# A second pair of tiles for the scan's solve, and context residual rows that stay on chip between output projection and second norm

## The chip, the core and the metric

The kernel runs on one core of a Trainium2 chip. TensorE multiplies matrices into PSUM, VectorE (DVE), ScalarE (ACT) and GpSimd (POOL) work on tiles of up to 128 partitions in on-chip memory, and SyncE (SP) issues nearly all transfers between that memory and DRAM. Each engine has a queue of its own that it takes in order, and an instruction waits until the tiles it reads are written and the buffer it writes is given back. The metric is the device time of one execution, the median of three runs.

## What is computed

Two layers of a generator's backbone. Each normalises the latent stream (1024 tokens) and the context stream (256 tokens), projects to four mixers (an RWKV-7 scan in both directions, pooling, a Fourier mixer, a convolution), concatenates and projects back, adds the gated result to the residual, normalises again, and applies a SwiGLU feed-forward block. The second layer needs no context output.

```python
def step(S, inp):                      # the scan, per token, head and direction
    w_t, kk_t, a_t, k_t, v_t = inp[:5]
    sa = jnp.einsum('bhvk,bhk->bhv', S, -kk_t)
    S = (S * w_t[:, :, None, :] + sa[..., None] * (kk_t * a_t)[:, :, None, :]
         + v_t[..., None] * k_t[:, :, None, :])
    y = jnp.einsum('bhvk,bhk->bhv', S, inp[5]) if with_out else None
    return S, y
...
    h = h + gt1 * _mix_and_project(ux, y_rwkv_x, *other)
    h = h + gt2 * _swiglu(_modulate(h, norm2_g[l], sh2, sc2), ffn_w_in[l], ffn_w_out[l])
    if not last:
        hc = hc + mc[2] * _mix_and_project(uc, y_rwkv_c, *other)
        hc = hc + mc[5] * _swiglu(_modulate(hc, norm2_g[l], mc[3], mc[4]), ffn_w_in[l], ffn_w_out[l])
```

All matrix products in FP32 are made of three matmuls of a high and a low half each.

## The kernel before

Activations lie as 128 channels by tokens: tb 0 and 1 are the latent's two halves of 512 tokens, tb 2 is the context's 256. The scan is cut into ten stages of 128 tokens a layer (two of context, eight of latent). A stage has a *preparation* (decays by L921 on POOL and the running sum L926 on VectorE, then L942, L947, L950, L956 and POOL's L943, L957, L971), the matmuls *rX* and their masking (L991, four a stage), and the *solve*. The solve inverts small triangular matrices: their entries go from the masked tiles to DRAM (eight stores to Ad, L995) and come back spread over all partitions into two tiles As[0] and As[1] (two loads, L1001). L1029 sets the diagonal on POOL, L1031 to L1035 start the solve on VectorE (As[0]) and POOL (As[1]), and L1043 to L1052 run over eight blocks on VectorE, blocks 0 to 3 from As[0], 4 to 7 from As[1]. The result goes by DRAM (Td, L1056, loaded by L1062) to the *merge* (L1102 and matmuls into pb), and then a chain of small matmuls (pc) and copies carries the state. In the text a stage n runs from the start of solve n to that of solve n + 1, and holds the preparation and the rX for solve n + 1.

Beside the scan `fill()` supplies work: the rest of the input projection, the Fourier mixer, and then the output projection `outp` for tb 2, 1 and 0 (the latent's without the scan's two channel blocks, which are added later). `outp` loads its y tiles from ymix (six for the latent, L1657), splits each into halves (cast L324 on ScalarE, subtraction L325 on POOL), and for each of eight column blocks loads weights and the residual r, runs 18 matmuls of 128x512 into a pf tile (24 of 256 columns for the context), evicts with gate and residual on VectorE (L1684) and stores to ho (L1685). After it `norm2c()` loads the context's eight finished rows back from ho into hc (L1348), takes their squares (L339) and their norm, and the context's feed-forward block follows.

What sets the order: the program is written as interleaved generators, and a scheduler then orders each engine's queue in a simulated time of its own. A tile is given a buffer from a pool; nearly all tiles of 128x512 or less come from one pool, t2, of 73 buffers, and an instruction can be placed only once a buffer is free in that reckoning. A ring `s.rg(R, name, depth)` holds `depth` t2 buffers through a scan.

Of the kernel before, what the change touches and what calls it, by code (L numbers as in the profile page):

```python
# [19 lines left out]
NK = 8  # L20
# [72 lines left out]
class _Kernel:  # L93
# [879 lines left out]
    def inner(s, R, F):  # L973

        nc = s.nc
# [5 lines left out]
        for d in range(2):  # L981
            s.lab(f"rX.{F.seg}{F.i}")
            psh = [s.ps(), s.ps()]
            for u in range(4):
                for h in range(2):
                    rows = slice(64 * h, 64 * h + 64)
# [8 lines left out]
                    nc.sync.dma_start(Ad[b, d, :, h].rearrange("u j i -> j u i"), W[r0:r0 + 32, :, 32 * b:32 * b + 32])  # L995
            yield

        As = [s.rg(R, f"As{a}", 1) for a in range(2)]
        Adf = Ad.rearrange("b d u h j i -> (b d u h) (j i)")
        for a in range(2):  # L1000
            nc.sync.dma_start(As[a], Adf[:, a * 512:(a + 1) * 512].unsqueeze(0).broadcast_to([4, 32, 512]))  # L1001
# [36 lines left out]
        for b in range(8):  # L1038
            x, r0, m = As[b // 4][:, :], 4 * b, b + 1
            o = (r0 % 16) * 32 + r0  # L1040
            with s.ahead(SPRI):
# [3 lines left out]
                n = 28 - r0  # L1045
# [210 lines left out]
    def run(s, nlayers):  # L1256
        nc = s.nc
# [26 lines left out]
        r = [s.norm_r(h, 0, sq="c2")]  # L1284
# [15 lines left out]
        for l in range(nlayers):  # L1300
            last = l == L - 1
# [22 lines left out]
            def fill():  # L1324
                for x in s.rest(l, R, acts, segs):
                    s.mod_step()
                    yield x
                assert not s.mods
                R.rest2 = True
                yield from s.four2(R, segs, swB, ymix)  # L1330
                while not R.sided or not (last or R.ctx):
                    yield None
                for tb in tbs[::-1]:
                    yield from s.outp(l, tb, hd, ho, ymix)
                if not last:
                    yield from norm2c()
                    for f in range(NC):
                        yield from s.ffn1_ctx(l, f, [a[2] for a in acts2], hid[f])

            def norm2c():  # L1340

                for _ in range(2):
                    yield
                s.lab("norm2")
                hc = s.rows(NK, ("c",))
                for k in range(NK):
                    h2[k][2] = hc[k][2]
                    nc.sync.dma_start(hc[k][2], ho[k][:, 1024:1280])  # L1348
                yield
                r = yield from s.rstd_g([h2[k][2] for k in range(NK)], 256, D, 0, False, "ps", lambda j: s.t2())  # L1350
                for k in range(NK):
                    acts2[k][2] = s.act_row(("c",))[2]
                for _ in s.norm_g(l, 1, h2, 2, acts2, r):
                    if _ % 2:
                        yield
# [289 lines left out]
            else:  # L1645
                break

    def outp(s, l, tb, hi_, ho, ymix):

        nc = s.nc  # L1650
        seg, _, n = TBS[tb]
# [20 lines left out]
        for cb in range(NK):  # L1672
            s.lab("outp")
            w = s.wload(s.I["wout"][l, cb], ks[0] * 128)
            r = s.t2()[:, :n]
            nc.sync.dma_start(r, hi_[cb][:, 512 * tb:512 * tb + n])
            ps = s.ps("pf")
            for i, ((wh, wl), (ah, al)) in enumerate(zip(w, acts)):
# [213 lines left out]
```

## Time and profile before

| what | us |
|---|---|
| median of three runs | 3343.46 (3340.38 to 3346.46) |
| the profiled execution's own time | 3351.38 |
| its span, first to last instruction | 3349.6 |
| TensorE busy, matmuls | 3000.7 |
| VectorE busy | 2109.8 |
| ScalarE busy | 1257.5 |
| POOL busy | 1385.8 |

The mean granted clock of TensorE was 0.911 of full speed. Times in the rows are counted from the start of the span. Layer 0's scan runs from about 370 to 910 us, layer 1's from about 2100 to 2600.

### The profile page before, as it was taken

To read this page: it belongs to the slowest core of one execution; us is meant where nothing else is said; L and a number is where in the kernel's file an instruction comes from. 1 tells how busy PE (TensorE), PEld (TensorE's weight loads), DVE (VectorE), ACT (ScalarE), POOL (GpSimd) and SP (SyncE) were. 2 spreads that over 40 slices of the span, in tenths; PEclk is the share of its full clock that TensorE was granted. 3 is DMA by queue.
4 is the path that set the end of the run, shared out by engine and by line. 5 is a ranking of instruction groups with operands and counts; after the bars stand their busy time and mean duration, and the time that the engine had idled before them with its cause. 6 is when DMAs were issued, how large, how long until landed. Compare 5 with 4: busy or idle time off the path is not lost.

```text
span 3349.6 us, 52386 instructions
## 1 busy us (share of the span) xinstructions
PE 3000.7 (90%) x18888; PEld 2410.5 (72%) x18888; DVE 2109.8 (63%) x3498; ACT 1257.5 (38%) x2575; POOL 1385.8 (41%) x1484
## 2 busy tenths in 40 slices
PE   6989997877889999999999978988877799999998
PEld 3657765766678888888888766756665588888787
DVE  6679666666374988644545598666665755554535
ACT  4446433443363222223212455333443433333212
POOL 2366224563168554435310064245550454545400
PEclk8989887787899999999999988987787799999999
DMA  7422344465455444337412212345553322224312
GB/s 265 165 92 97 102 117 136 124 174 156 144 190 164 149 132 151 125 98 233 139 35 78 87 53 90 117 134 139 156 159 88 128 92 79 82 89 164 123 39 78
DMA packets 375818, 415.48 MB, mean 124 GB/s; under 512 B 115587, under 2 KB 214916, under 8 KB 375558
## 3 DMA queue, kind: packets, MB, share of 16 engines
q1 hardware_dynamic: 375558, 412.13, 39.4%
q8 instruction: 149, 2.44, 0.3%
q14 instruction: 111, 0.91, 0.1%
HBM read 306.49 MB, written 100.27 MB: 121 GB/s over the span
## 4 chain that ended last, share of the span: by engine, by line
PE 55%; DVE 14%; DMA 9%; issue 3%; SPq 1%; ACT 1%; POOL 1%; DVEq 0%; POOLq 0%; ACTq 0%
PE pc L153 17%; PE ps L153 17%; PE pb L153 14%; PE pf L153 8%; DMA t<-Ad 3%; DVE c L532 2%; DMA Td<-t 1%; DVE t L1050 1%; DVE t L947 1%; DVE t L1043 1%; DVE f L325 1%; DVE t L956 1%; DVE t L1469 1%; DMA t<-ho 1%; DVE t L1493 1%
## 5 line engine op out<-in xcount | busy, mean ns | idle before, releaser
L153 PE MATMUL pc<-t,f 128*128 128x512 f32 (+1 forms) x3108 | 754.4, 392 | 41.3 <-ACT t L427 16.0
L153 PEld LDWEIGHTS pc<-t,f 128*128 128x128 f32 x3108 | 581.6, 195 | 182.9 <-ACT t L427 20.5
L153 PE MATMUL ps<-t,f 128*128 128x512 f32 (+1 forms) x2094 | 517.0, 393 | 18.4 <-ACT t L324 7.7
L153 PE MATMUL pb<-t,f 128*128 128x512 f32 (+1 forms) x2094 | 470.5, 370 | 8.4 <-ACT t L1468 4.9
L153 PEld LDWEIGHTS ps<-t,f 128*128 128x128 f32 x2094 | 390.8, 190 | 99.8 <-ACT t L324 8.2
L153 PEld LDWEIGHTS pb<-t,f 128*128 128x128 f32 x2094 | 370.4, 190 | 78.8 <-ACT t L1468 6.0
L1515 ACT CAST f<-c 128x512 fp32r<-128x512 f32 x316 | 196.0, 621 | 536.7 <-PE ps L153 132.0
L1517 POOL TENSOR_TENSOR f<-c,f 128x512 fp32r<-128x512 f32 x135 | 186.5, 1381 | 426.2 <-ACT f L1515 411.7
L153 PE MATMUL pf<-t,f 128*128 128x512 f32 (+2 forms) x1500 | 314.2, 364 | 14.2 <-DVE t L1044 4.0
L324 ACT CAST f<-m 128x512 fp32r<-128x512 f32 (+1 forms) x236 | 134.7, 576 | 436.3 <-PE pb L153 226.4
L153 PEld LDWEIGHTS pf<-t,f 128*128 128x128 f32 (+1 forms) x1500 | 249.5, 198 | 61.4 <-ACT f L324 4.4
L530 POOL TENSOR_TENSOR c<-c,cp 128x352 f32<-128x352 f32 (+2 forms) x168 | 183.3, 1092 | 145.9 <-ACT c L523 71.3
L1517 DVE TENSOR_TENSOR f<-c,f 128x512 fp32r<-128x512 f32 x181 | 158.6, 878 | 134.8 <-ACT f L1515 134.4
L153 PE MATMUL pf<-c,f 128*128 128x512 f32 (+1 forms) x704 | 200.5, 416 | 30.0 <-DVE t L1684 20.3
L325 POOL TENSOR_TENSOR t<-c,t 128x512 fp32r<-128x512 f32 (+1 forms) x110 | 135.1, 1266 | 173.8 <-PE ps L153 99.5
L153 PE MATMUL ps<-t,t 64*128 64x128 f32 (+2 forms) x1032 | 159.9, 341 | 38.9 <-DVE t L956 23.4
L532 DVE SCALAR_TENSOR_TENSOR c<-c,dv,c 128x352 f32<-128x352 f32 (+2 forms) x238 | 190.5, 829 | 2.0
L153 PEld LDWEIGHTS ps<-t,t 64*128 64x128 f32 (+1 forms) x1032 | 133.6, 231 | 60.4 <-issue 20.4
L153 PEld LDWEIGHTS pc<-t,t 128*64 128x64 f32 (+2 forms) x2484 | 124.6, 161 | 71.8 <-issue 28.6
L153 PE MATMUL pc<-t,t 128*64 128x64 f32 (+3 forms) x2484 | 156.2, 258 | 20.9 <-DMA t<-t 11.8
L153 PEld LDWEIGHTS pf<-c,f 128*128 128x128 f32 x704 | 131.5, 214 | 60.1 <-issue 19.1
L261 DVE SCALAR_TENSOR_TENSOR cp<-m,sc,cp 128x512 f32<-128x512 f32 x140 | 137.5, 1003 | 43.0 <-DMA m<-in_wmod 42.3
(256 smaller groups left out, 4731.3 us busy)
## 6 DMA issues: line engine op xcount, KB each, us to landing
c<-in_ffin SPq DMA_DIRECT2D x176, 256.0 KB
m<-in_wmod SPq DMA_DIRECT2D x116, 256.0 KB
t<-rw SPq DMA_DIRECT2D x232, 128.0 KB
hid<-t SPq DMA_DIRECT2D x88, 256.0 KB
c<-hid SPq DMA_DIRECT2D x88, 256.0 KB
m<-in_ffout SPq DMA_DIRECT2D x80, 256.0 KB
t<-in_wmod SPq DMA_DIRECT2D x76, 256.0 KB
m<-in_win SPq DMA_DIRECT2D x64, 256.0 KB
```

The lines of the kernel that those rows point to most:

```text
L153: s.nc.tensor.matmul(o, l, r, start=start, stop=stop)
L261: nc.vector.scalar_tensor_tensor(acc[t], w, sc, acc[t], ALU.mult, ALU.add)
L324: r = s.nc.scalar.copy(hi, src)
L325: (eng or s.lo_eng).tensor_tensor(lo, src, hi.bitcast(F32), ALU.subtract)
L530: nc.gpsimd.tensor_tensor(g, g, t_, ALU.add)
L532: nc.vector.scalar_tensor_tensor(a, w[:, j:j + m], tap(j), a, ALU.mult, ALU.add)
L947: nc.vector.scalar_tensor_tensor(KRv[:, :, p, 0, 1:64], k2[:, :, p, 1:64], -2.0, P2[:, :, p, 0:63], ALU.mult, ALU.mult)
L956: nc.vector.tensor_tensor(BKv[rows, :, :, 1 - h, :], cv(kd)[rows], cv(iP)[rows], ALU.mult)
L1043: nc.vector.tensor_tensor(tv, at(x, o, [0, m], [1, 4], [32, 4]), at(T_, r0, [32, m], [0, 4], [1, 4]), ALU.mult)
L1050: nc.vector.tensor_tensor(tv, at(x, o + 4, [0, m], [1, n], [32, 4]), at(T_, r0, [32, m], [0, n], [1, 4]), ALU.mult)
L1515: nc.scalar.copy(hi, x)
L1517: (nc.gpsimd if s.nw % 7 in LOP else nc.vector).tensor_tensor(lo, x, hi.bitcast(F32), ALU.subtract)
```

## The change

`inner` takes As[0] and As[1] from rings of depth 2 in place of 1: two more t2 buffers are held through each scan. In `fill()` the context's four tiles of two rows each (`hc`) are taken before the output projection, and `outp` for the context writes its residual straight into them, in place of eight r tiles of its own; `norm2c` then finds the rows there, without the eight loads and the `yield` behind them. The store to ho stays. Lines behind the change count one less (L1684 becomes L1683, L1657 becomes L1656).

```diff
@@ -995,7 +995,7 @@
                     nc.sync.dma_start(Ad[b, d, :, h].rearrange("u j i -> j u i"), W[r0:r0 + 32, :, 32 * b:32 * b + 32])
             yield
 
-        As = [s.rg(R, f"As{a}", 1) for a in range(2)]
+        As = [s.rg(R, f"As{a}", 2) for a in range(2)]
         Adf = Ad.rearrange("b d u h j i -> (b d u h) (j i)")
         for a in range(2):
             nc.sync.dma_start(As[a], Adf[:, a * 512:(a + 1) * 512].unsqueeze(0).broadcast_to([4, 32, 512]))
@@ -1330,8 +1330,12 @@
                 yield from s.four2(R, segs, swB, ymix)
                 while not R.sided or not (last or R.ctx):
                     yield None
+                if not last:
+                    hc = s.rows(NK, ("c",))
+                    for k in range(NK):
+                        h2[k][2] = hc[k][2]
                 for tb in tbs[::-1]:
-                    yield from s.outp(l, tb, hd, ho, ymix)
+                    yield from s.outp(l, tb, hd, ho, ymix, hc if tb == 2 else None)
                 if not last:
                     yield from norm2c()
                     for f in range(NC):
@@ -1342,11 +1346,6 @@
                 for _ in range(2):
                     yield
                 s.lab("norm2")
-                hc = s.rows(NK, ("c",))
-                for k in range(NK):
-                    h2[k][2] = hc[k][2]
-                    nc.sync.dma_start(hc[k][2], ho[k][:, 1024:1280])
-                yield
                 r = yield from s.rstd_g([h2[k][2] for k in range(NK)], 256, D, 0, False, "ps", lambda j: s.t2())
                 for k in range(NK):
                     acts2[k][2] = s.act_row(("c",))[2]
@@ -1645,7 +1644,7 @@
             else:
                 break
 
-    def outp(s, l, tb, hi_, ho, ymix):
+    def outp(s, l, tb, hi_, ho, ymix, rows=None):
 
         nc = s.nc
         seg, _, n = TBS[tb]
@@ -1672,7 +1671,7 @@
         for cb in range(NK):
             s.lab("outp")
             w = s.wload(s.I["wout"][l, cb], ks[0] * 128)
-            r = s.t2()[:, :n]
+            r = rows[cb][tb] if rows else s.t2()[:, :n]
             nc.sync.dma_start(r, hi_[cb][:, 512 * tb:512 * tb + n])
             ps = s.ps("pf")
             for i, ((wh, wl), (ah, al)) in enumerate(zip(w, acts)):
```

The number of instructions on the compute engines is the same, and SP issues eight transfers fewer. The order moves, chiefly in layer 0's stages 8 and 9. First VectorE at the start of solve 9, before: t_721 is As[0] and t_722 As[1], t_855 the tile of solve 8, pf a finished column block of the output projection (none stands here), ps an rX.

```order
L1044 TENSOR_REDUCE t_855_4076<-t_855_4076 128x7x4
L991 TENSOR_TENSOR t_892_4311<-ps_7131,cv 128x512
L1050 TENSOR_TENSOR t_855_4076<-t_722_3289,t_855_4076 128x112
L1051 TENSOR_REDUCE g_6839<-t_855_4076 128x28
L1052 TENSOR_TENSOR t_855_4076<-t_855_4076,g_6839 128x7x4
L1043 TENSOR_TENSOR t_855_4076<-t_722_3289,t_855_4076 128x128
L1044 TENSOR_REDUCE t_855_4076<-t_855_4076 128x8x4
L1031 TENSOR_TENSOR g_7303<-t_721_3288 128x4x2
L1032 TENSOR_TENSOR t_721_3288<-t_721_3288,g_7303 128x4
L1033 TENSOR_TENSOR g_7303<-t_721_3288 128x4x2
L1034 TENSOR_TENSOR t_721_3288<-t_721_3288,g_7303 128x4
L1035 TENSOR_TENSOR t_721_3288<-t_721_3288,g_7303 128x4x2
```

Here solve 9 follows the last instruction of solve 8 directly. And with the change, at the same place; t_663, t_682, t_683, t_688, t_689, t_776 and t_777 are tiles of the last preparation, t_1211, t_1227 and t_1250 the residual tiles of tb 1's first three blocks.

```order
L947 SCALAR_TENSOR_TENSOR t_777_3615<-t_595_2613,t_683_3064 128x2x63 x2
L950 TENSOR_TENSOR t_777_3615<-t_596_2616,t_683_3064 128x4x64
L942 TENSOR_TENSOR t_663_2960<-t_663_2960,t_594_2610 128x256 x2
L956 TENSOR_TENSOR t_688_3091<-t_663_2960,t_682_3063 64x2x2x64 x2
L956 TENSOR_TENSOR t_689_3092<-t_663_2960,t_682_3063 64x2x2x64 x2
L1683 SCALAR_TENSOR_TENSOR t_1211_6813<-pf_6815,mod_78,t_1211_6813 128x512
L1102 STREAM_TRANSPOSE t_936_4580<-t_835_3981 128x256
L1683 SCALAR_TENSOR_TENSOR t_1227_6945<-pf_6947,mod_78,t_1227_6945 128x512
L1683 SCALAR_TENSOR_TENSOR t_1250_7156<-pf_7158,mod_78,t_1250_7156 128x512
L1031 TENSOR_TENSOR g_7301<-t_721_3288 128x4x2
L1032 TENSOR_TENSOR t_721_3288<-t_721_3288,g_7301 128x4
L1033 TENSOR_TENSOR g_7301<-t_721_3288 128x4x2
```

The last preparation has moved ahead of solve 9 as a whole, and three evictions of the output projection and a merge's transposition (L1102) stand between it and the solve's first instruction.

Second SP's queue, before, at the stores for solve 8; t_1183 and t_1186 are the last two of tb 1's six y tiles (the other four stand earlier), t_594, t_595 and t_596 inputs of a preparation, Ad_6667 is solve 8's.

```order
L1120 DMA t_892_4311<-t_777_3615 64x4x64
L1657 DMA t_1183_6590<-ymix_853 128x512
L876 DMA t_594_2610<-rw_894 128x2x128 x2
L876 DMA t_595_2613<-rw_895 128x2x128
L965 DMA ks_6560<-t_692_3144 128x512
L1685 DMA ho_862<-t_1166_6467 128x256
L876 DMA t_595_2613<-rw_895 128x2x128
L876 DMA t_596_2616<-rw_896 128x2x128 x2
L1657 DMA t_1186_6594<-ymix_854 128x512
L1201 DMA yb_6665<-t_884_4284 128x512
L995 DMA Ad_6667<-t_812_3895 32x4x32 x2
L995 DMA Ad_6667<-t_814_3897 32x4x32 x2
```

Here all six y loads stand ahead of the stores that solve 8 waits for. With the change, the place in SP's queue at which the y tiles of tb 1 are loaded; Ad_7092 is solve 9's, Td_7176 solve 8's result, t_906 the tile that its merge reads, t_1169 to t_1184 are the six y tiles.

```order
L995 DMA Ad_7092<-t_892_4311 32x4x32 x2
L995 DMA Ad_7092<-t_894_4313 32x4x32 x2
L1001 DMA t_721_3288<-Ad_7092 128x1x512
L1001 DMA t_722_3289<-Ad_7092 128x1x512
L1056 DMA Td_7176<-t_857_4078 4x256x32
L1656 DMA t_1169_6572<-ymix_849 128x512
L1656 DMA t_1172_6576<-ymix_850 128x512
L1062 DMA t_906_4382<-Td_7176 32x8x32
L1656 DMA t_1175_6580<-ymix_851 128x512
L1062 DMA t_906_4382<-Td_7176 32x8x32 x3
L1656 DMA t_1178_6584<-ymix_852 128x512
L1656 DMA t_1181_6588<-ymix_853 128x512
```

The six y loads have moved from ahead of solve 8's stores to behind solve 9's As loads. Their buffers are those of two tiles of the scan's weights, of the mask that L926 reads, and of inputs of the preparation (L942, L943 and L950 read them), which are given back by the last preparation, that for solve 10. Of 18 matmuls a column block, 76 and 50 stand between the starts of consecutive stages' dg transposes (L1008) in stages 8 and 9 before, and 0 and 116 with the change; behind them 162 before and 172 with the change. With the change the matmuls of stage 9's second rX stand behind 109 of the 116, the last 55 of them, two merges and two state chains behind the third block's last matmul. Before about 400 us, from 1100 to 2100 us and behind 2600 us the order is the same; in layer 1's scan L991 moves back by up to 17 of a solve's 42 VectorE instructions in five stages.

## Rows read from the trace of the kernel before

**Rows 1.** The page: busy time by engine, and the chain that ended last by line.

```profile
PE 3000.7 (90%) x18888; PEld 2410.5 (72%) x18888; DVE 2109.8 (63%) x3498; ACT 1257.5 (38%) x2575; POOL 1385.8 (41%) x1484
...
PE pc L153 17%; PE ps L153 17%; PE pb L153 14%; PE pf L153 8%; DMA t<-Ad 3%; DVE c L532 2%; DMA Td<-t 1%; DVE t L1050 1%; DVE t L947 1%; DVE t L1043 1%; DVE f L325 1%; DVE t L956 1%; DVE t L1469 1%; DMA t<-ho 1%; DVE t L1493 1%
```

**Rows 2.** Waits from 370 to 915 us: engine, line, what for; total us, times, longest.

```profile
DVE g L1031 <- DMA t<-Ad: 62.8, 8, 11.2
```

**Rows 3.** Timeline, VectorE and SP's queue, stage 3: start, us, line, [idle before <- releaser].

```profile
528.22 0.29 DVE L1044 TENSOR_REDUCE t<-t 128x32 f32<-128x128 f32 x1
...
543.00 1.82 SPq L995 DMA_DIRECT2D Ad<-t  x4
...
546.45 1.12 SPq L1001 DMA_DIRECT2D t<-Ad  x2
...
554.83 0.17 DVE L1031 TENSOR_TENSOR g<-t 128x8 f32<-128x8 f32 x1 [9.15 <-DMA t<-Ad]
```

**Rows 4.** Timeline, VectorE and SP's queue, stage 4, which has no output projection.

```profile
565.34 2.67 DVE L956 TENSOR_TENSOR t<-t,t 64x256 f32<-64x256 f32 x4
...
577.00 0.68 DVE L991 TENSOR_TENSOR t<-ps,cv 128x512 f32<-128x512 f32 x1
...
581.84 0.56 SPq L1001 DMA_DIRECT2D t<-Ad  x1
...
585.10 0.56 SPq L1001 DMA_DIRECT2D t<-Ad  x1
...
591.25 0.10 DVE L1031 TENSOR_TENSOR g<-t 128x8 f32<-128x8 f32 x1
```

**Rows 5.** Timeline, VectorE and SP's queue, from the start of solve 8 to that of solve 10.

```profile
721.15 0.17 DVE L1031 TENSOR_TENSOR g<-t 128x8 f32<-128x8 f32 x1 [9.55 <-DMA t<-Ad]
...
728.34 2.24 DVE L926 TENSOR_TENSOR_SCAN t<-t,t 128x512 f32<-128x512 f32 x1
...
772.98 0.17 DVE L1031 TENSOR_TENSOR g<-t 128x8 f32<-128x8 f32 x1 [11.10 <-DMA t<-Ad]
...
818.15 0.17 DVE L1031 TENSOR_TENSOR g<-t 128x8 f32<-128x8 f32 x1 [7.78 <-DMA t<-Ad]
```

**Rows 6.** Timeline, VectorE, the last preparation of layer 0, in stage 9.

```profile
777.85 1.23 DVE L926 TENSOR_TENSOR_SCAN t<-t,t 128x512 f32<-128x512 f32 x1 [2.34 <-POOL t L921]
...
782.79 1.55 DVE L942 TENSOR_TENSOR t<-t,t 128x256 f32<-128x256 f32 x2
...
785.96 2.66 DVE L956 TENSOR_TENSOR t<-t,t 64x256 f32<-64x256 f32 x4
```

**Rows 7.** Timeline, POOL, one subtraction for the low half of a y tile.

```profile
714.10 1.27 POOL L325 TENSOR_TENSOR c<-t,c 128x512 fp32r<-128x512 f32 x1 [9.30 <-ACT c L324]
```

**Rows 8.** Windows: us, busy (x count) by engine, clock; all, then tile pf; last the chain.

```profile
721.10:773.00 51.90, 41.59 (x406) 32.03 (x406) 31.59 (x65) 18.61 (x50) 28.62 (x43) 0.90 0.63 184
...
773.00:818.20 45.20, 35.91 (x370) 27.72 (x368) 31.41 (x70) 15.84 (x40) 20.99 (x32) 0.77 0.55 158
...
840.00:890.00 50.00, 50.00 (x465) 36.52 (x461) 18.55 (x29) 20.86 (x50) 16.06 (x16) 0.99 0.49 149
...
711.70:760.60 48.90, 23.42 (x76) 15.47 (x76) 2.93 (x4) 0.00 (x0) 0.87 0.65 179
...
760.60:806.40 45.80, 14.27 (x50) 10.02 (x50) 1.48 (x2) 0.00 (x0) 0.78 0.57 159
...
884.61 4.99 PE pf L153 x21
```

**Rows 9.** Waits of VectorE in layer 1's scan, 2100 to 2620 us.

```profile
DVE t L991 <- PE ps L153: 26.8, 10, 7.7
```

**Rows 10.** Timeline, SP's queue and ScalarE, the start of the context's second norm.

```profile
913.86 3.74 SPq L1348 DMA_DIRECT2D t<-ho x8
...
917.65 1.70 ACT L339 ACTIVATE t<-t 128x256 f32<-128x256 f32 x4 [0.40 <-DMA t<-ho]
...
921.71 0.42 ACT L339 ACTIVATE t<-t 128x256 f32<-128x256 f32 x1 [1.14 <-DMA t<-ho]
```

## The prediction

> **What bounds the kernel now.** I read the page first: TensorE is busy for 90% of the span, and matmuls lead the chain that ended last [rows 1]. So a wait is worth something only where TensorE runs out of work, and a gap closed elsewhere is given back. The change reaches the two RWKV scans (370 to 910 us and 2100 to 2600 us) and the start of the context's second norm (914 us), so I read the waits of the first scan next: VectorE waits at the head of 8 of its 10 solves, 62.8 us in all, for the load of the solve's matrices [rows 2]. That is the wait at which a second pair of As tiles seems to aim. I number the solves of a scan 1 to 10. The timeline of one such wait shows what it hangs on [rows 3]: the last read of As by the solve before ends at 528.5; the last four stores to Ad are issued from 543.00; the load into As is issued at 546.45, right behind them, and VectorE goes on at 554.83. The tile had been free for 18 us when the load was issued. The load waits for its data to be in DRAM, not for a tile.
>
> **The second As pair, by itself.** Where the buffer does count is the second of the two loads: at 581.84 the first is issued, at 585.10 the second, while the solve before still reads that tile [rows 4]. Of such split pairs the two scans hold five, none wider than these 3.3 us. But blocks 0 to 3 of a solve read only As[0], and VectorE reached the solve at 591.25, after the first tile. So I take 0 for this edit's direct gain; its other end is 5 x 3.3 = 16 us gained.
>
> The Trainium skill ("Trainium Kernel Development and Optimization", Best Practices) advises double buffers to overlap DMA with compute; by that each split would close, which is the second rival below, and [rows 3] speak against it, since nothing is left to overlap there.
>
> **What the second pair costs: order.** All t2 tiles come from one pool of 73, and the scheduler places instructions by when a buffer is free in its own reckoning. Two of them are now held through each scan. The count of instructions on the compute engines is the same; what moves is seen in the order. The largest move: the six y tiles of the latent's first output projection (tb=1) are loaded, before, ahead of solve 8's stores to Ad; now they stand behind solve 9's As loads and wait for tiles that the last preparation (the one that feeds solve 10) gives back. So that projection's matmuls, 76 and 50 in the two stages [rows 8], come to 0 and 116 (18 a column block, counted in the order). And on VectorE three evictions (L1683) of that projection stand ahead of the first instruction of solve 9, where before there was none.
>
> Now the sum, in us from solve 8's start (721.15, its first row after the wait). Before, solve 9 begins 51.8 later and solve 10 97.0 later [rows 5].
>
> Stage 8 gets faster. With no projection in it, I price it by the stage that has none [rows 4]: the preparation's last L956 ends at 568.0, the last L991 9.7 later, the first As load is issued another 4.2 later, and it lands some 9 later (VectorE idle 9.15 at such a load [rows 3]). L926 came 7.2 after the start of stage 8 [rows 5], and from L926 to the end of L956 it is 10.8 [rows 6]: last L956 at 18, L991 at 28, As load at 32, landed at 41. By itself that is 11 us gained.
>
> But solve 9 can't begin then, since VectorE is in order and the evictions stand first. Their chain: POOL's L921 of the last preparation stands behind its part of solve 9, which waits for As; from solve start to L926 was 4.9 [rows 6], so L926 at 46 here; L942 ends 6.5 after L926 began, at 52 [rows 6]. The y loads that wait for L950, L942 and POOL's L943 of this preparation are issued at 50 to 53 and land some 3 later (the nearest row: the first of eight loads is used 3.8 after its issue [rows 10]). Six casts on ScalarE and six subtractions on POOL follow, the latter 1.27 each [rows 7], with POOL's eight L957 and L971 between them, on half as many elements or fewer (estimated at half the time, 5): 8 + 5 = 13 from 53 on, so the last one ends at about 67. Blocks 0 and 1 are interleaved on TensorE and mostly done by then; left are some 5 matmuls of them and 18 of block 2, with a merge of 16 small ones between. At the dense rate of 0.238 us (21 in 4.99 [rows 8]) that is 5.5, at half of it 11; the granted clock was 0.77 in stage 9, where TensorE had gaps, and 0.99 where it had none [rows 8], and here it will have idled for long. Third eviction at about 75: solve 9 begins 23 us later than before. Bounds: 66 (all y early) to 82.
>
> Stage 9 then holds what two stages held. Between the third block and the matmuls of stage 9's second rX (which feed the last L991) TensorE's queue has 55 projection matmuls, 13.1 us, and merges and state chains of two solves, where a stage holds one. Outside the projection TensorE was busy 41.6 - 23.4 = 18 and 35.9 - 14.3 = 22 us in stages 8 and 9 [rows 8] (the windows differ by a few us, so these are estimates); half of that for each of two chains is 20. So rX at 75 + 33 = 108, L991 at 109, load issue 4, landing 9: solve 10 at 122 against 97.0, 25 late. If stage 9 lasted only as long as a stage without projection (36.4 [rows 3, 4]) from the early bound 66, it would be 102: 5 late. If it lasted 45.2, as before, from 82: 127, 30 late. I take 23, a bit under the middle estimate, because some of the queue's projection matmuls fall into waits of the chain.
>
> Does the tail give it back? From 840 to 890 TensorE is busy 50.00 of 50 us at clock 0.99 [rows 8], and the order there is the same with ten more projection matmuls (172 for 162). No: what solve 10 is late by, the scan ends late by.
>
> **Smaller moves.** In layer 0's stage 3 the next preparation goes behind the solve: it may put off its L991s by 0 to 4 us (about the stretch from the stores to the load in [rows 3]), I take 1. In layer 1 the L991s come later in five stages, mostly behind the solve's end, by -1 to +8 us in all; VectorE already waited 26.8 us at ten L991s there [rows 9], which hides most, so I take 1.
>
> **The residual rows on chip.** The eight loads hc <- ho are issued from 913.86 in 3.74 us of SP's queue; the squares on ScalarE wait for them at 917.65 (0.40) and again at 921.71 (1.14), the last of the eight [rows 10]. Without them the squares could begin when the last ho row is written, and L1377's second pair of loads moves up. The norm is followed by TensorE at once and that stretch is poorly filled. At least 0 (ScalarE and SP have other work there), at most 5; I take 3 gained, near the 3.74. Four tiles are held from the context's projection on; four fewer are needed as its r tiles, so the pool is none the worse.
>
> Sum: +23 + 1 + 1 - 3 = +22. The profiled run took 3351.38 us, 7.9 over the median of 3343.46; a difference carries over, so 3343.5 + 22 = **3365**.
>
> **The rivals.** (1) *VectorE is not held*: the y tiles arrive early, so that the three evictions cost nothing. Then solve 9 begins at 41 (11 us gained), stage 9 takes the moved matmuls, (116 - 50) x 0.238 = 15.7, of which 45.2 - 35.9 = 9.3 of TensorE's idle time hide most: -11 + 6 - 3 = -8, about 3335; if all are hidden, 3329. It decides where the third eviction ends before about 52, the time at which solve 9 began before; each us beyond is a us lost. For it: y loads that wait for nothing but TensorE's last reads (two of the six). Against it: the other four wait for the last preparation, which itself waits for As, and that alone is 46. (2) *The second pair closes the splits*: up to 16 + 3 gained, 3325 to 3340; against it [rows 3, 4]. (3) *All absorbed*: TensorE idled for 10 + 9 us in stages 8 and 9 [rows 8], as much as the late solve takes, so that the full tail starts no later, and only the loads' gain stays: 3340, within the bound of no change. (4) *Solves of layer 1 too*: the late L991s each delay a stage, at 2 to 3 us in five stages with the layer 0 term at its low end of 5: 3343.5 + 5 + 13 - 3 = 3358; this differs from my forecast in place, not in sign. (5) *The change doesn't do what it says*: the pair is never used two at a time, so that only the order moves; that is my forecast's own reading of the first edit.
>
> **How the numbers follow.** My forecast, a slower kernel by solve 9 held on VectorE: 0.57 (its own range 3350 to 3382); rival 4: 0.08; rival 1: 0.14; rival 2: 0.07; rival 3: 0.14. About 0.2% (6.7 us) is what a measurement of this kernel can tell from no change. So slower by more: 0.65; within: 0.14; faster: 0.21. The range takes in the forecast's whole range and the nearer part of rivals 1 and 3: 3333 to 3383.
>
> **What would show it.** In the profile after: solve 9's first L1031 right behind three L1683, some 70 to 80 us after solve 8's, and ended by TensorE's pf, not by a DMA; POOL's six subtractions late, about 50 to 67; the clock of TensorE at half in the stretch before; solve 10 115 to 127 after solve 8; the wait of [rows 2] smaller by the As load that solve 9 no longer waits for, without any gain from it; no loads between the L1377 pairs. Solve 9 begun within 60 us would make the forecast wrong, and so would a scan of layer 0 that ends no later though solve 9 is late.

## The result: 43 us slower, under half of it where I expected it, the rest mostly where I had put 1 us

The changed kernel takes 3385.31 us (3378.99 to 3389.02, four runs) against 3341.92 for the kernel before: a ratio of 1.0128, 95% interval 1.0105 to 1.0152, or 35 to 51 us. I had forecast 3365 with a range that ended at 3383. The direction was right, the size was not.

The profiles must be compared with one caution. In the profiled execution of the kernel before, a single subtraction on VectorE took 11.20 us, where its neighbours take 0.67, and TensorE waited for it.

```profile
3097.18 13.65 POOL L325 TENSOR_TENSOR t<-c,t 128x512 fp32r<-128x512 f32 x11
...
3100.18 11.20 DVE L325 TENSOR_TENSOR f<-m,f 128x512 fp32r<-128x512 f32 x1 [3.54 <-ACT f L324]
...
3111.43 4.63 PE L153 MATMUL pc<-t,f 128*128 128x512 f32 x10 [7.17 <-DVE f L325]
3111.96 0.68 DVE L325 TENSOR_TENSOR f<-m,f 128x512 fp32r<-128x512 f32 x1
```

Above, the kernel before, timeline (start us, us, engine, line, tile, idle before). That is more than the 7.9 us by which its profiled run lay over its median, and the larger part of why the two spans differ by 27.6 us only; the changed kernel's profiled run, 3378.99 us, also lies 6.3 us under its own median. Up to that instruction the changed kernel's trace is 38.7 us behind. Following the same instruction through both traces, the lag grows like this:

| at | lag, us |
|---|---|
| layer 0, solve 8 | 1.6 |
| solve 9 | 11.4 |
| solve 10 | 9.8 |
| end of layer 0's scan | 12.5 |
| dense feed-forward of layer 0, up to layer 1's first solve | 17.3, 16.5 |
| layer 1, solve 10 | 31.4 |
| end of layer 1's scan | 36.3 |
| dense feed-forward of layer 1 | 38.7 |

The page hardly shows this: the busy times are those of before within 3 us [rows 1], and in the chain by line no share moves by more than 2 points (pf 8 to 10%, L532 2 to 4%).

```profile
PE 2998.4 (89%) x18888; PEld 2409.3 (71%) x18888; DVE 2112.8 (63%) x3498; ACT 1258.5 (37%) x2575; POOL 1387.0 (41%) x1484
...
PE pc L153 17%; PE ps L153 16%; PE pb L153 14%; PE pf L153 10%; DVE c L532 4%; DMA t<-Ad 3%; DVE t L1050 1%; DMA Td<-t 1%; DVE t L1043 1%; DVE t L1492 1%; DVE t L1052 1%; DVE t L947 1%; DVE g L1051 1%; DVE t L956 1%; DVE t L401 1%
```

**Layer 0, stage 8.** The changed kernel's timeline, VectorE, POOL and SP's queue, from solve 8 (722.75) to solve 9, answers to [rows 5 to 7]:

```profile
722.75 0.17 DVE L1031 TENSOR_TENSOR g<-t 128x8 f32<-128x8 f32 x1 [9.85 <-DMA t<-Ad]
...
744.34 0.68 DVE L991 TENSOR_TENSOR t<-ps,cv 128x512 f32<-128x512 f32 x1
...
747.00 1.16 SPq L1001 DMA_DIRECT2D t<-Ad  x2
...
752.86 0.13 POOL L1029 MEMSET t<- 128x16 f32 x1 [13.04 <-DMA t<-Ad]
...
757.13 1.23 DVE L926 TENSOR_TENSOR_SCAN t<-t,t 128x512 f32<-128x512 f32 x1 [7.88 <-POOL t L921]
...
761.28 3.10 SPq L1656 DMA_DIRECT2D t<-ymix  x3
...
773.90 1.29 POOL L325 TENSOR_TENSOR cp<-t,c 128x512 fp32r<-128x512 f32 x1
...
776.67 0.75 DVE L1683 SCALAR_TENSOR_TENSOR t<-pf,mod,t 128x512 f32<-128x512 f32 x1 [10.31 <-DMA t<-hd]
777.70 0.71 DVE L1683 SCALAR_TENSOR_TENSOR t<-pf,mod,t 128x512 f32<-128x512 f32 x1
783.67 0.75 DVE L1683 SCALAR_TENSOR_TENSOR t<-pf,mod,t 128x512 f32<-128x512 f32 x1 [5.26 <-issue]
784.34 0.29 DVE L1031 TENSOR_TENSOR g<-t 128x8 f32<-128x8 f32 x1
```

It is the chain that I forecast, link by link, with one link more: the first eviction's wait ended with a residual load (`DMA t<-hd`), at about the time of its block's last matmuls (776.6). The last L991 is 22.3 us after solve 8 (39.2 before), and As is on chip for solve 9 at 752.86, 30.1 after it. But POOL goes on to the last preparation only then, so L926 begins at 757.13, the last three y tiles are issued from 761.28, the last subtraction ends at 775.2, and the third eviction ends at 784.4. Solve 9 follows at once, with no wait for a DMA: its data had been there for 31 us. The windows of stages 8 and 9 (busy time and count for TensorE, weight loads, VectorE, ScalarE, POOL, then the clock) answer to [rows 8]:

```profile
722.75:784.30 61.55, 33.90 (x198) 26.86 (x200) 33.56 (x76) 15.04 (x36) 37.85 (x60) 0.64 0.48 141
784.30:828.00 43.70, 42.16 (x538) 32.54 (x536) 26.31 (x59) 22.30 (x57) 12.33 (x16) 1.00 0.67 190
```

TensorE has 33.9 us of work in 61.6, at a granted clock of 0.64 on average. Then it is full.

**Layer 1, stage 7** (from its solve 7 to its solve 8) is the longest of its stages 4 to 8, which all grew, and grew most: 53.6 us for 48.8. The changed kernel's timeline, POOL, TensorE and VectorE:

```profile
2406.49 1.39 POOL L1158 TENSOR_TENSOR gg<-t,pcs 64x256 f32<-64x256 f32 x2
2420.11 0.41 POOL L1018 TENSOR_SCALAR t<-cv 128x256 f32<-128x256 f32 x1 [12.24 <-DMA Td<-t]
2423.40 0.13 POOL L1029 MEMSET t<- 128x16 f32 x1 [2.88 <-DMA t<-Ad]
2425.89 0.13 POOL L1029 MEMSET t<- 128x16 f32 x1 [2.36 <-DMA t<-Ad]
...
2426.70 1.26 POOL L325 TENSOR_TENSOR c<-t,c 128x512 fp32r<-128x512 f32 x1
...
2428.01 1.65 PE L153 MATMUL pf<-c,f 128*128 128x512 f32 x3 [8.30 <-POOL c L325]
...
2467.25 1.29 DVE L991 TENSOR_TENSOR t<-ps,cv 128x512 f32<-128x512 f32 x2 [7.63 <-PE ps L153]
...
2476.99 0.17 DVE L1031 TENSOR_TENSOR g<-t 128x8 f32<-128x8 f32 x1 [5.37 <-DMA t<-Ad]
```

And the kernel before, POOL and VectorE, at the same work:

```profile
2395.16 1.27 POOL L325 TENSOR_TENSOR c<-t,c 128x512 fp32r<-128x512 f32 x1 [7.72 <-ACT c L324]
2400.54 0.13 POOL L1029 MEMSET t<- 128x16 f32 x1 [4.11 <-DMA t<-Ad]
...
2438.27 0.68 DVE L991 TENSOR_TENSOR t<-ps,cv 128x512 f32<-128x512 f32 x1
```

Before, the first subtraction for the last output projection (tb 0) stands ahead of solve 7's memset on POOL and runs 5 us before it. Changed, it stands behind L1018, which waits 12.24 us, and behind both memsets, which wait for As: it runs 3 us after solve 7 begins. TensorE, with the projection's matmuls at the head of its queue, idles 8.30 us for it and then has projection matmuls in front of rX: the last L991 ends 45.2 us after the solve's start, and 38.5 before. It is the same fault as in layer 0: work that TensorE needs stands on an in-order queue behind the wait for As.

TensorE's waits for these subtractions from 2380 to 2490 us, the kernel before and then the changed kernel:

```profile
PE pf L153 <- POOL c L325: 3.7, 2, 3.3
...
PE pf L153 <- POOL c L325: 8.3, 1, 8.3
```

So this fault adds some 5 us of wait, and it isn't all of the stage's length. Of the twelve kernels traced here only the changed one has that first subtraction behind solve 7's memset, and yet stage 7 takes 51.7 us in e1 and 52.4 in e4 (below), where the subtraction runs 5 to 6 us ahead of the solve. e4 loses nothing in all: its stage 9 is 4.2 us shorter than before. One longer stage is not yet a loss.

**The context's norm.** With the loads gone the squares run without a wait, 2.55 us for all eight, and end 9.7 us behind the scan's last L1246 and not 12.4 [rows 10]. But the next step takes what was gained. ScalarE, the changed kernel:

```profile
929.38 2.55 ACT L339 ACTIVATE t<-t 128x256 f32<-128x256 f32 x8
936.99 0.31 ACT L353 ACTIVATE t<-ps,cv 128x64 f32<-128x64 f32 x1 [5.06 <-PE ps L153]
```

The kernel before:

```profile
924.61 0.31 ACT L353 ACTIVATE t<-ps,cv 128x64 f32<-128x64 f32 x1 [2.49 <-PE ps L153]
```

L353 waits for TensorE's sums, which stand in its queue among matmuls of the latent's projection: 5.06 us now for 2.49 before. It begins 14.8 us behind the scan's end, where it was 14.9. The five other runs below that keep the rows on chip (e2, e5, e6, e9, e10) say the same: the eight squares run in 2.55 us without a wait, and L353 begins 14.5 to 15.8 us behind the scan's end.

### The profile page after: what moved, and what is told of

It reads as the page before. It is cut to its first block, busy times and chain, and to the rows that moved or that the text cites. A ratio compares the mean times of both kernels' runs of the same rounds, so it can differ in the third digit from the quotient of the medians.

```text
span 3377.2 us, 52385 instructions
## 1 busy us (share of the span) xinstructions
PE 2998.4 (89%) x18888; PEld 2409.3 (71%) x18888; DVE 2112.8 (63%) x3498; ACT 1258.5 (37%) x2575; POOL 1387.0 (41%) x1484
## 4 chain that ended last, share of the span: by engine, by line
PE 58%; DVE 21%; DMA 10%; issue 4%; POOL 2%; ACT 2%; SPq 2%; DVEq 0%; POOLq 0%; ACTq 0%
PE pc L153 17%; PE ps L153 16%; PE pb L153 14%; PE pf L153 10%; DVE c L532 4%; DMA t<-Ad 3%; DVE t L1050 1%; DMA Td<-t 1%; DVE t L1043 1%; DVE t L1492 1%; DVE t L1052 1%; DVE t L947 1%; DVE g L1051 1%; DVE t L956 1%; DVE t L401 1%
## 5 line engine op out<-in xcount | busy, mean ns | idle before, releaser
L153 PE MATMUL pc<-t,f 128*128 128x512 f32 (+1 forms) x3108 | 750.2, 390 | 39.1 <-ACT t L427 14.5
L153 PE MATMUL pf<-t,f 128*128 128x512 f32 (+2 forms) x1500 | 312.5, 363 | 16.5 <-DMA f<-eo 5.3
L153 PE MATMUL ps<-t,t 64*128 64x128 f32 (+2 forms) x1032 | 169.8, 355 | 62.3 <-DVE t L956 36.6
L153 PEld LDWEIGHTS ps<-t,t 64*128 64x128 f32 (+1 forms) x1032 | 143.5, 244 | 87.2 <-issue 33.4
L532 DVE SCALAR_TENSOR_TENSOR c<-c,dv,c 128x352 f32<-128x352 f32 (+2 forms) x238 | 188.3, 819 | 2.0
```

The costliest lines, as they stand in the source:

```text
L153: s.nc.tensor.matmul(o, l, r, start=start, stop=stop)
L532: nc.vector.scalar_tensor_tensor(a, w[:, j:j + m], tap(j), a, ALU.mult, ALU.add)
```

## The experiments

All lengths below are from the first L1031 of each solve in the trace of the run; "1 to 10" is the time from a layer's first solve to its last. Ratios are to runs of the kernel before on the same chips.

| run | ratio (95%) | stage 8, 9 of layer 0 | layer 0, 1 to 10 | layer 1, 1 to 10 |
|---|---|---|---|---|
| before | 1 | 51.8, 45.2 | 429 | 403 |
| changed | 1.0128 (1.0105 to 1.0152) | 61.6, 43.7 | 437 | 418 |
| e1 pair alone | 1.0079 (1.0050 to 1.0108) | 51.5, 44.8 | 429 | 410 |
| e2 rows alone | 1.0062 (1.0042 to 1.0081) | 47.0, 53.4 | 433 | 411 |
| e3 one tile held | 1.0036 (1.0019 to 1.0053) | 48.7, 46.2 | 429 | 401 |
| e4 pair in layer 1 | 1.0005 (0.9986 to 1.0024) | 50.6, 43.8 | 421 | 400 |
| e5 both, pair in layer 0 | 1.0047 (1.0029 to 1.0066) | 60.9, 43.0 | 433 | 404 |
| e6 both, y in place | 1.0060 (1.0041 to 1.0079) | 52.5, 45.3 | 433 | 405 |
| e7 before, y in place | 0.9982 (0.9965 to 0.9999) | 38.0, 45.7 | 415 | 401 |
| e8 loads twice | 1.0025 (1.0011 to 1.0040) | 52.3, 45.2 | 430 | 406 |
| e9 subtractions on VectorE | 1.0085 (1.0068 to 1.0103) | 61.2, 43.4 | 442 | 408 |
| e10 rows, y in place | 1.0022 (1.0012 to 1.0033) | 41.5, 43.4 | 415 | 401 |

How far one trace can be trusted: before, e4 and e8 have the same order on VectorE, ScalarE and POOL through layer 0's scan, and their stages 8 agree within 1.7 us, the whole scan within 9 (429, 421, 430). The changed kernel, e5 and e9 share an order there too: 437, 433 and 442, with stage 8 at 61.6, 60.9 and 61.2. So the longer stage 8 is far clear of jitter, and the longer scan is clear of it by three traces against three, though not by one against one. A profiled run also lies up to 12 us off its kernel's median (e6: 3353.49 for 3365.30), so what a trace shows need not add up to the ratio.

**e1 and e2: one edit each.**

e1, against the kernel before:

```diff
-        As = [s.rg(R, f"As{a}", 1) for a in range(2)]
+        As = [s.rg(R, f"As{a}", 2) for a in range(2)]
```

e2, against the changed kernel:

```diff
-        As = [s.rg(R, f"As{a}", 2) for a in range(2)]
+        As = [s.rg(R, f"As{a}", 1) for a in range(2)]
```

> The second As pair alone; the context's rows are loaded back as before. In its order the projection's matmuls in layer 0's stages 8 and 9 are 61 and 47 (before 76 and 50, changed kernel 0 and 116), and in layer 1 the L991 of stages 14 and 16 come behind their solves as in the changed kernel. Theory (two buffers fewer spoil the order, the pair is the main taker): solve 9 of layer 0 is late by at most 4 us, layer 1's scan is late by 10 to 20 us, in all 3355 to 3370 us. Rival (the rows held on chip are what costs, the pair is free): within 5 us of the kernel before, some 3342. Rival (the pair closes the waits for As): under 3336.

> The residual rows kept on chip alone; one As pair. Order: 32 and 97 projection matmuls in stages 8 and 9 of layer 0, and in layer 1 the L991 later in stages 13 and 14 only. Theory (two takers, the pair the larger): solve 9 late by 2 to 6 us, the norm 0 to 3 us earlier, layer 1 late by 0 to 6: 3342 to 3354. Rival (the rows are what costs): 3375 to 3390, with solve 9 about 10 us late.

Measured: 3363.31 us and 3362.32. Each edit alone costs about half of the whole, 0.79% and 0.62% for 1.28%. e1 is as expected, though its layer 1 lost 7 us between the solves, less than thought. e2 was a miss: with one As pair and no edit in layer 1 at all, layer 1 still loses 8 us between its solves, and stage 9 of layer 0 takes 53.4 us. So neither "the pair alone is what costs" nor "the rows alone are what costs" holds; each changes the order, and each costs.

**e3 and e4: a taker of a buffer that is no pair, and a pair where it disturbs little.**

e3, against the kernel before:

```diff
+        Zs = [s.rg(R, f"Z{a}", 1) for a in range(1)]
...
+        for z in Zs:
+            nc.gpsimd.tensor_scalar(z[:, 0:8], Tt[:, 0:8], 1.0, 0.0, ALU.mult, ALU.add)
```

e4, against the kernel before (l is the layer, 0 or 1):

```diff
+            R.da = 1 + l
...
-        As = [s.rg(R, f"As{a}", 1) for a in range(2)]
+        As = [s.rg(R, f"As{a}", R.da) for a in range(2)]
```

> The kernel before, with one more t2 tile that is only held through each scan: eight columns are written by POOL in each stage (20 small writes, under 0.2 us each) and never read. Order: 60 and 42 projection matmuls in stages 8 and 9, the L991 in layer 1's stages 14 and 16 behind the solve, much as with the second pair alone. Theory (the loss is that of buffers and order, whatever takes them): 3350 to 3368, about as the second pair alone. Rival (the loss is the second pair's own, its loads and waits): within 5 us of the kernel before, 3342.

> The second As pair in layer 1's scan alone, nothing else. The order is that of the kernel before up to 2200 us. Theory (layer 1's own buffers spoil its order): everything is as before up to 2200 us, then 8 to 20 us lost by the end of the scan: 3350 to 3362. Rival (layer 1's loss is carried over from layer 0's other order): within 4 us of before, 3342.

Measured: 3349.63 us (e3), about half the loss of e1 and just under the range that I expected; a tile that is never read, with its 20 small writes, costs 0.19 to 0.53%. That this is the cost of its order is an inference: between its solves e3's trace loses nothing (429 and 401 us), and it doesn't show where the time goes. e4: 3342.00 for 3342.00. The theory that layer 1's own buffers spoil its order falls, and "carried over" alone does not hold either (e5). e4 also shows the direct worth of the second pair. In layer 1 of the kernel before the two As loads of a solve are issued 1.4 to 3.2 us apart in four stages and 0.6 in the others; in e4 they are 0.6 apart in eight stages, and 1.0 and 1.8 in two. So the pair does close most splits. But VectorE's wait for As in layer 1's scan doesn't shrink, here first the kernel before and then e4 (total us, times, longest):

```profile
DVE g L1031 <- DMA t<-Ad: 62.7, 9, 11.1
...
DVE g L1031 <- DMA t<-Ad: 66.3, 9, 13.3
```

Nothing is gained, as [rows 3] said. The Trainium skill's advice to double-buffer ("Trainium Kernel Development and Optimization", Best Practices) finds nothing to overlap here.

**e5: layer 1 put back.** Both edits, the pair in layer 0 only. The order of layer 1's scan on VectorE, ScalarE and POOL is then again that of the kernel before.

Against the changed kernel:

```diff
+            R.da = 2 - l
...
-        As = [s.rg(R, f"As{a}", 2) for a in range(2)]
+        As = [s.rg(R, f"As{a}", R.da) for a in range(2)]
```

> Both edits, but the second As pair in layer 0's scan only. In its order layer 0 is that of the changed kernel (0 and 116 projection matmuls in stages 8 and 9) and layer 1 that of the kernel before, row for row in the positions of L991 and the counts of projection matmuls. Theory (the loss is two separate pieces, each that of an order): layer 0 as in the changed kernel, 10 to 18 us lost up to 2100 us, nothing lost in layer 1: 3352 to 3362. Rival (layer 1 is late because layer 0 is, or by its buffers): 3375 to 3388, as the changed kernel.

Measured: 3360.50 us, 1.0047: some 16 us of the 43 are left. Its solve 9 is held as in the changed kernel. VectorE, e5:

```profile
717.43 0.17 DVE L1031 TENSOR_TENSOR g<-t 128x8 f32<-128x8 f32 x1 [10.32 <-DMA t<-Ad]
...
777.68 0.75 DVE L1684 SCALAR_TENSOR_TENSOR t<-pf,mod,t 128x512 f32<-128x512 f32 x1 [5.27 <-issue]
778.34 0.23 DVE L1031 TENSOR_TENSOR g<-t 128x8 f32<-128x8 f32 x1
```

That is 60.9 us for the changed kernel's 61.6. And layer 1, with the order of before, has the stages of before to within 0.9 us: 41.1, 45.3, 38.9, 49.4, 41.6 and 39.7 from solve 4 on, against 40.8, 44.8, 39.2, 48.8, 40.7 and 39.6. A late start does not make layer 1 slow. So the loss is two pieces, each an order: about 16 us (10 to 22 by the interval) in layer 0 and behind it, and the rest, some 27, in layer 1.

**e6 and e7: y tiles that take no buffer.** The y tile is loaded into the tile that its low half is later written to.

In `outp`; e6 has it on the changed kernel, e7 on the kernel before:

```diff
-            y = s.t2()[:, :n]
-            nc.sync.dma_start(y, ymix[k][:, 512 * tb:512 * tb + n])
...
                 a = s.t2(F32R, "c2"), s.t2(F32R, "c2" if k < 6 else "cp")
+            y = a[1].bitcast(F32)
+            nc.sync.dma_start(y, ymix[k][:, 512 * tb:512 * tb + n])
```

> The changed kernel, with the y tiles of the output projection loaded straight into the tile that their low half is then written to, so that the y loads take no t2 buffer and wait for no buffer of the last preparation. Order: 36 and 87 projection matmuls in stages 8 and 9; the last preparation and three evictions still stand ahead of solve 9. Theory (solve 9 was held because the y loads waited for the last preparation): solve 9 comes 52 us or less after solve 8, in place of 61.6, and layer 0 loses under 5 us. In layer 1 the last L991 comes behind all 42 of the solve's instructions in five of six stages from the fourth on, so that 8 to 15 us are lost there by the rows of the first experiments: 3350 to 3362 in all. Rival (solve 9 is late by the order of VectorE alone, wherever y comes from): about 60 us again, and 3365 to 3380.

> The kernel before with the same in-place y tiles as the run above, one As pair, rows loaded back. Order: 61 and 45 projection matmuls in stages 8 and 9, in layer 1 the last L991 behind 38, 42, 32, 42, 42 and 33 of the solve's instructions in the stages from the fourth on (kernel before: 32, 42, 30, 42, 42, 31). Theory (the place of L991 sets a stage's length): layer 0 within 4 us, layer 1 0 to 6 us longer, 3340 to 3350. Rival (six buffers more at the projection are worth something): under 3336.

Measured: e6 3365.30 us, 20 us less than the changed kernel. Solve 9 comes 52.5 us after solve 8, about as the theory had it, and layer 0 loses 4 us. The total is a miss, over the 3350 to 3362 expected, and one that its trace, 12 us faster than its median, doesn't explain. VectorE, e6:

```profile
723.67 0.17 DVE L1031 TENSOR_TENSOR g<-t 128x8 f32<-128x8 f32 x1 [10.98 <-DMA t<-Ad]
...
765.09 1.23 DVE L926 TENSOR_TENSOR_SCAN t<-t,t 128x512 f32<-128x512 f32 x1 [12.78 <-POOL t L921]
766.23 0.73 DVE L1683 SCALAR_TENSOR_TENSOR t<-pf,mod,t 128x512 f32<-128x512 f32 x1
767.23 0.71 DVE L1683 SCALAR_TENSOR_TENSOR t<-pf,mod,t 128x512 f32<-128x512 f32 x1
775.50 0.75 DVE L1683 SCALAR_TENSOR_TENSOR t<-pf,mod,t 128x512 f32<-128x512 f32 x1
776.17 0.38 DVE L1031 TENSOR_TENSOR g<-t 128x8 f32<-128x8 f32 x1
```

The evictions still stand first, and still hold the solve, but they are ready 9 us earlier. The wait of the y loads was worth those 9 us. As is on chip for solve 9 at 758.50 (POOL's first L1029), so the place of the evictions still holds the solve for 17.7 us. In e7, where none stands there, solve 9 begins 38.0 us after solve 8, and what ended its wait is As.

```profile
719.91 0.17 DVE L1031 TENSOR_TENSOR g<-t 128x8 f32<-128x8 f32 x1 [10.41 <-DMA t<-Ad]
...
757.91 0.17 DVE L1031 TENSOR_TENSOR g<-t 128x8 f32<-128x8 f32 x1 [7.78 <-DMA t<-Ad]
```

Above, VectorE, e7. In e6 the order of layer 1 changed too, and its stage 7 fell from 53.6 to 44.3 us. e7 is a miss too, to the good side: 3338.13 us for 3340 to 3350, and layer 0's scan 13.6 us shorter where I expected it within 4. It gains 13.8 us in stage 8 and ends 6 us faster in all (0.01 to 0.35%): where that stage got shorter, 23 projection matmuls more are left behind the scan's last rX (186 for 163, counted in the traces), 5.5 us at 0.238, and the lead at the end of the scan is 8.7 us and at the dense feed-forward 5.2.

**e8: the loads doubled**, on the kernel before.

```diff
                     nc.sync.dma_start(hc[k][2], ho[k][:, 1024:1280])
+                    nc.sync.dma_start(hc[k][2], ho[k][:, 1024:1280])
```

> The kernel before with the eight loads of the context's rows issued twice, 16 in place of 8. Up to and through layer 0's scan its order is that of the kernel before; in layer 1 the order differs all the same (the last L991 behind 28, 44, 28, 42, 39 and 31). Theory (the loads hide behind TensorE, so taking them away gained nothing): the stretch from the end of layer 0's scan to the first feed-forward layer within 2 us of the kernel before, and 3338 to 3350 in all. Rival (the loads cost their issue time, 3.74 us for eight): that stretch 3 to 5 us longer.

Measured: 3351.08 us; the stretch behind layer 0's scan is 6.8 us longer, so my theory fails in this direction, and the 3 to 5 us of its rival were too few. ScalarE, e8:

```profile
928.70 0.42 ACT L339 ACTIVATE t<-t 128x256 f32<-128x256 f32 x1 [0.67 <-DMA t<-ho]
...
929.56 0.31 ACT L353 ACTIVATE t<-ps,cv 128x64 f32<-128x64 f32 x1 [0.44 <-PE ps L153]
```

The last square ends 17.6 us behind the scan's end and L353 starts at 18.0, with hardly a wait for TensorE left. So the eight loads and TensorE's queue end within 2 us of each other in the kernel before: eight loads more cost 3.1 us at L353, eight fewer gain 0.1. Where the other 3.7 us of that stretch come from isn't shown. Layer 1's order changed here as well, by eight loads in layer 0.

**e9: the subtractions of layer 1 off POOL.**

Against the changed kernel:

```diff
-            s.pin(s.split(y, *a))
+            s.pin(s.split(y, *a, eng=nc.vector if l else None))
```

> The changed kernel, with the subtractions of layer 1's y tiles on VectorE in place of POOL (twelve of 0.7 us each, by the row of the 128x512 subtraction on VectorE). Layer 0's order is that of the changed kernel. Theory (in layer 1's stage from the seventh solve to the eighth, 53.6 us in the changed kernel and 48.8 before, TensorE starves for y tiles whose subtractions stand on POOL behind the wait for As): that stage comes down to 50 us or less, and layer 1's loss of 15 us between its first and last solve to under 10: 3366 to 3380. Rival (the stage is long because its matmuls are many and L991 stands behind the solve): 52 us or more, 3380 to 3390.

Measured: 3370.81 us, within the theory's range. Layer 1 takes 408 us between its solves for 418 (403 before), its stage 7 31.3 us and stage 6 47.8, together 79.1 for 94.8 in the changed kernel and 88.0 before. VectorE, e9:

```profile
2383.32 0.17 DVE L1031 TENSOR_TENSOR g<-t 128x8 f32<-128x8 f32 x1 [3.28 <-DMA t<-Ad]
...
2417.02 0.69 DVE L325 TENSOR_TENSOR c<-t,c 128x512 fp32r<-128x512 f32 x1 [0.55 <-ACT c L324]
...
2431.10 0.57 DVE L1031 TENSOR_TENSOR g<-t 128x8 f32<-128x8 f32 x1
```

The first subtraction now runs 14 us ahead of solve 7, not behind its wait. This is for the reading of stage 7, with one limit: the edit moves other work of layer 1 as well, so that stage 3 grows from 44.8 to 53.5 us and stage 4 shrinks from 44.2 to 27.3, and the ten us gained between the solves are those of the whole edit.

**e10: the part that removes work, on the better y tiles.** The changed kernel with one As pair and the edit of e6.

> The kernel before with the residual rows kept on chip and the y tiles in place, one As pair: the edit of the changed kernel that removes work, without the pair. Order: 69 and 34 projection matmuls in stages 8 and 9 (before 76 and 50), the last L991 behind 37 of the solve's instructions in both; in layer 1 much as the kernel before with y in place. Theory (only the order matters): stage 8 about 38 to 46 and stage 9 about 44 us, layer 1 as in that run: 3328 to 3342, the fastest of all. Rival (rows kept on chip cost, whatever the order): 3350 or more.

Measured: 3348.18 us, 1.0022: a miss, though the solves ran as expected (stages 8 and 9 take 41.5 and 43.4 us, layer 1 401). At solve 10 of layer 0 it leads by 13.2 us; at the end of the scan, with 185 projection matmuls behind the last rX for 163, by 7.4; at the dense feed-forward by 1.0. The scan's lead is given back to matmuls that TensorE has to do all the same, and keeping the rows on chip adds no lead.

The total lies nearer to the rival, rows that cost whatever the order. e10 differs from e7 by the rows alone and is 0.40% slower; e2 is 0.62% slower than before, and the changed kernel 0.49% slower than e1. So the rows cost 0.4 to 0.6% in each of three pairs of runs. Each pair differs in its order too, and no run here tells the one from the other. No version tried here beats the kernel before by more than e7's 0.18%.

## Why the prediction was right in direction and wrong in size

- **What bounds: right.** The wait for As is a wait for stores [rows 3], and the second pair, which closed most splits, shortened none (e4).
- **Solve 9 held by three evictions: right as a mechanism, its size wrong.** I had solve 9 late by 23 us, and it was late by 9.8. I had As on chip at 41 us, L926 at 46, the last subtraction at 67, solve 9 at 75; measured 30, 34, 52 and 61.6. The links behind As took 31.5 us for my 34; the head did not hold, because I priced stage 8 by the stage without projection, 28 us to the last L991, and it was 22.3, with 2 us from there to the load's issue and not 4, and 6 from the issue to the memset and not 9. The 9 was misread: it is VectorE's idle time at a load [rows 3], and in the same rows the solve begins 8.4 us after the load's issue. (The 3.8 us of [rows 10] are those of the second square; the first began at 916.84, 3.0 after the issue.) So the signs came in kind and not in size: solve 9 behind three evictions, but at 61.6 us and not 70 to 80, solve 10 at 105.2 and not 115 to 127, the subtractions from 39 to 52 us and not 50 to 67.
- **Stage 9: wrong by 3 us.** I had 47 us; it took 43.7, TensorE busy for 42.16 of it at clock 1.00. The low clock that I had reckoned with fell in stage 8 (0.64), where TensorE had little to do. Both terms together: +23 forecast, +8.2 measured from solve 8 to solve 10, and the traces of the same orders agree: from solve 8 to solve 10 they have 105.2, 103.9 and 104.7 us (changed, e5, e9) and 97.0, 94.4 and 97.6 (before, e4, e8).
- **The tail gives nothing back: right.** The lag goes from 9.8 to 12.5 us, the ten more matmuls being 2.4, which the sum had left out. e7 and e10 show the same from the other side.
- **The rows on chip, -3: wrong.** The step that failed is that "the squares could begin when the last ho row is written" and that the time so gained passes on to the norm. The squares did end 2.7 us earlier, but TensorE's queue decided when the norm went on. From the scan's end to the dense feed-forward the changed kernel loses 4.8 us. e4, with the order of before in that stretch, loses 2.2; e5 and e9, with the changed kernel's order there, lose 5.5 and 6.6. So in this order the stretch got some 4 us longer, where I had 3 us gained. e1, without the rows on chip, loses 3.8 there as well, and what makes up the loss isn't shown.
- **Layer 1, +1: the step that broke the range.** I had seen that the L991s move back by up to 17 of 42 instructions in five stages, priced it at -1 to +8, and took 1 since VectorE waits there anyhow [rows 9], "which hides most". That is the step that failed. The wait is for TensorE, and it did not hide the move but grew with it. VectorE's waits in layer 1's scan, the changed kernel:

```profile
DVE t L991 <- PE ps L153: 38.5, 15, 7.6
```

  That is 38.5 us at 15 L991s for 26.8 at ten; e5, with the order of before, has 28.4 at ten. Stages 4 to 8 lengthened by 3.4, 0.7, 2.0, 4.8 and 4.0 us, 14.9 in all, and 7.3 more came behind the last solve, where I had +1. By the runs it is some 27 us (1.0128 against e5's 1.0047). One thing that I did not look at was POOL's order there: in layer 0 I had followed the y tiles through POOL's queue, in layer 1 I looked at VectorE's rows alone. It is a part and not the whole: TensorE's waits for the y tiles' subtractions in layer 1's scan are 11.7 us for 5.3, and e1 and e2 lose 7 and 8 us there without a longer wait at L991 (20.3 and 25.7).
- **Rival 4** named the place, at a chance of 0.08, and its 13 us in five stages were near the 14.9; it went with a small loss in layer 0 and nothing behind the last solve, and so gave 3358. Rivals 1 to 3 did not occur.

Left open: why an edit in layer 0 alone (e2, e8) changes the order of layer 1, which lies inside the scheduler's reckoning; which moves make up the 14.9 us between layer 1's solves beyond POOL's part, and the 7.3 behind the last one (e4, which loses nothing in all, has 7.7 there); whether the rows cost by themselves or by their order; and the loss that the pair and the rows bring together in layer 1 but the pair held in layer 1 alone (e4) does not, which I can only put down to two different orders.

## What to carry to other kernels

Where a scheduler sets each engine's order by buffers, one more buffer held can be an edit of the whole order: compare the orders, and price each stage whose order moved, on every engine and not only on the one that seems to wait. Look for work that a busy engine needs and that now stands, on an in-order queue, behind a wait of another chain; bound its price by that wait, not by the work. And ask of a removed load who is ready next: here TensorE's queue was, so that taking eight loads away gained nothing while adding eight cost 3 us.

## What the runs showed that I had not expected

The same order can repeat closely: all nine stages between layer 1's solves in e5 repeat those of the kernel before within 0.9 us, though they start 12 us later. It is no rule, since in layer 0 three traces of one order differ by up to 4.3 us in a stage (stage 1: 71.4, 69.7 and 74.0 us in the changed kernel, e5 and e9).

And one instruction can stall a whole execution. The subtraction of 11.20 us in the profiled run of the kernel before lies within a run of eleven subtractions on POOL, from 3097.18 to 3110.83, and ends 0.55 us behind them. In that trace the 120 subtractions of this shape on VectorE with POOL idle beside them take at most 0.70 us, and 19 with POOL busy all through have a median of 0.98 us, at most 1.89. The changed kernel has the same run of eleven with no such stall:

```profile
3137.17 15.62 POOL L325 TENSOR_TENSOR t<-c,t 128x512 fp32r<-128x512 f32 x11
...
3138.74 1.54 DVE L325 TENSOR_TENSOR f<-m,f 128x512 fp32r<-128x512 f32 x1 [3.40 <-ACT f L324]
```

In all twelve traces VectorE's subtractions take longer beside POOL's work (medians of 0.77 to 1.22 us for 0.68). That this also made the one long stall is not shown.
